# A trunk's FFN up-projections as seven products of quarters in place of eight

## The chip, the cores and the metric

The kernel runs on one core of a Trainium2 chip, as one launch. The metric is device time in microseconds, the median of several executions. TensorE multiplies matrices into PSUM; VectorE and ScalarE do element-wise work and can read PSUM; GpSimd does element-wise work on SBUF; SyncE issues the loads of the weights.

## The reference

The trunk has four layers on 512 tokens of 1024 features: retention, conv FFN, stick-breaking attention, conv FFN, each behind an RMS norm and added to x, with a norm at the end. All is float32. The change touches the conv FFN alone:

```python
def _conv_ffn(h, w_up, conv_w, conv_b, w_down):
    u = h @ w_up
    u = lax.conv_general_dilated(u, conv_w[:, None, :].astype(u.dtype), window_strides=(1,),
                                 padding=[(CONV_W - 1, 0)], ...,
                                 feature_group_count=2 * D_FF) + conv_b
    gate, val = jnp.split(u, 2, axis=-1)
    return (jax.nn.silu(gate) * val) @ w_down
```

`w_up` is 1024 x 5632 (gate and value, 2816 columns each), `w_down` 2816 x 1024, and the convolution is causal, of width 3, on every feature by itself.

## The kernel before, in words

Activations lie feature-major: a tile has 128 features in its partitions and the 512 tokens in its columns. x is eight such tiles. Every operand of a large product is held as a pair, `hi` (float32 cut to 12 significant bits) and `lo` (what is left), and a product is three matmuls, hi·hi, hi·lo and lo·hi (`mm3`, lines 106 to 111).

Weights come as a stream of chunks of 128 x 1024 floats (`chunk`, lines 94 to 104): SyncE loads a `raw` tile (three buffers), ScalarE casts `hi`, VectorE subtracts to get `lo` (four buffers each). A projection of a chunk (`proj`, line 134) takes 8 k tiles x 3 matmuls of 512 columns into one PSUM tile `acc` (three buffers).

An FFN (`ffn`, lines 394 to 403) has 22 feature tiles of gate and 22 of value. `first4` (line 117) does the first four of these 44 tiles with the k tiles outermost, so that they start while the norm is still being summed; half-way, `rsqrt` (line 183) makes `r`, the norm's factor per token, which ends with VectorE's RECIPROCAL on line 192. The factor is multiplied in behind the product: `up` (line 367) has VectorE multiply the PSUM tile by `r`, ScalarE take the last tap of the convolution and VectorE the two others (lines 374 to 377). `ffn_act` (line 380) has ScalarE's Silu, VectorE's product and a `split` into hi and lo. After 8, 16 (or 14) and 22 (or 18) features a part of the down-projection follows (`down`, lines 388 to 392): 8 output tiles of up to 24 matmuls of 512 columns, each added to x by VectorE.

The program is written in this order, and a scheduler sets the order on each engine at build time, by its own priorities and by which buffers come free; on the chip each engine then works strictly in that order. Waits are semaphores between engines. GpSimd does next to nothing: constants, and one-column memsets in the attention.

## Time and profile before

| | |
|---|---|
| time, median of 3 runs | 1389.64 us (1389.42 to 1390.57) |
| span of the profiled execution | 1387.6 us |
| that execution's own time | not listed apart; the runs' median is 2.0 us above the span |
| TensorE matmul busy | 1375.7 us, 99% of the span, 6668 instructions |
| VectorE busy | 940.1 us, 68%, 1282 instructions |
| ScalarE busy | 592.6 us, 43%, 867 instructions |
| GpSimd busy | 6.8 us, 69 instructions |
| read from HBM | 123.67 MB, 91 GB/s over the span |
| mean granted TensorE clock | 0.998 of full speed |

Times in the profile are microseconds unless marked ns. PE is TensorE's matmul row, PEld its weight loads, DVE is VectorE, ACT ScalarE, POOL GpSimd, SP SyncE. L103 is line 103 of the kernel. Matmul durations overlap: a matmul's row lasts longer than the distance to the next one's start, so their cost is read from starts. "out<-in" are the program's tile names without their numbers.

### The profile page before, as it was taken

What the parts mean: (1) busy time and instruction counts of PE and PEld (TensorE: products, weight loads), DVE (VectorE), ACT (ScalarE), POOL (GpSimd) and SP (SyncE); (2) the same over time, 40 slices, a digit from 0 to 9 for tenths busy, and PEclk for the clock granted to TensorE, in tenths of its full rate; (3) what the DMA queues carried; (4) which work ended last, traced back from release to release, by engine and by line L of the source; (5) the groups of instructions that cost most, each with busy time, mean ns of one, the idle gap of its engine ahead of it and who ended that gap; (6) DMA issues with size and microseconds to landing.
All of it is one profiled execution on the core that took longest, in us unless ns stands there. A gap on an engine that the chain in (4) does not pass through costs nothing.

```text
span 1387.6 us, 17028 instructions
## 1 busy us (share of the span) xinstructions
PE 1375.7 (99%) x6668; PEld 1140.9 (82%) x6668; DVE 940.1 (68%) x1282; ACT 592.6 (43%) x867; POOL 6.8 (0%) x69
## 2 busy tenths in 40 slices
PE   9999999999999999999999999999999999999997
PEld 7888888888888888888888888787788888888887
DVE  7774564654669773676367779889788753765765
ACT  5443332433355441443244655554355432433434
POOL 0000000000000000000000000000000000000000
PEclk9999999999999999999999999999999999999999
DMA  8233133131324333233322431120133233223221
GB/s 266 72 93 105 56 106 107 50 102 61 91 84 127 94 93 105 92 98 100 91 84 69 122 92 52 57 72 25 56 105 123 92 94 103 84 86 120 72 95 62
DMA packets 41025, 126.88 MB, mean 91 GB/s; under 512 B 4592, under 2 KB 6768, under 8 KB 40944
## 3 DMA queue, kind: packets, MB, share of 16 engines
q1 hardware_dynamic: 39424, 124.45, 29.0%
q10 hardware_dynamic: 1520, 1.33, 0.3%
q8 instruction: 53, 0.87, 0.3%
q14 instruction: 28, 0.23, 0.1%
HBM read 123.67 MB, written 2.10 MB: 91 GB/s over the span
## 4 chain that ended last, share of the span: by engine, by line
PE 96%; DVE 3%; ACT 0%; issue 0%; DMA 0%; DVEq 0%; ACTq 0%
PE acc L109 22%; PE acc L111 22%; PE acc L110 22%; PE att L109 8%; PE att L110 8%; PE att L111 8%; PE one L484 2%; PE z L458 1%; PE tp L476 1%; DVE cs L464 1%; DVE lo L103 1%; DVE tt L430 0%; DVE tt L427 0%; PE one L188 0%; PE one L223 0%
## 5 line engine op out<-in xcount | busy, mean ns | idle before, releaser
L102 ACT CAST hi<-raw 128x1024 fp32r<-128x1024 f32 (+2 forms) x253 | 244.6, 968 | 389.2 <-PE acc L110 182.0
L110 PE MATMUL acc<-xl,hi 128*128 128x512 f32 x960 | 374.6, 390 | 0.0
L111 PE MATMUL acc<-xh,lo 128*128 128x512 f32 x960 | 374.2, 390 | 0.0
L109 PE MATMUL acc<-xh,hi 128*128 128x512 f32 x960 | 374.2, 390 | 0.0
L103 DVE TENSOR_TENSOR lo<-raw,hi 128x1024 fp32r<-128x1024 f32 (+2 forms) x253 | 281.9, 1115 | 46.6 <-ACT hi L102 38.0
L111 PEld LDWEIGHTS acc<-xh,lo 128*128 128x128 f32 x960 | 180.2, 188 | 38.0 <-issue 0.5
L109 PEld LDWEIGHTS acc<-xh,hi 128*128 128x128 f32 x960 | 180.2, 188 | 36.6 <-issue 0.5
L110 PEld LDWEIGHTS acc<-xl,hi 128*128 128x128 f32 x960 | 180.3, 188 | 36.0
L377 DVE SCALAR_TENSOR_TENSOR tt<-tt,vec,tt 128x511 f32<-128x511 f32 (+1 forms) x176 | 131.2, 747 | 4.0 <-ACT tt L375 1.1
L374 DVE TENSOR_TENSOR tt<-acc,rr 128x512 f32<-128x512 f32 x80 | 55.0, 687 | 85.5 <-PE acc L111 85.5
L161 DVE TENSOR_TENSOR x<-x,att 128x512 f32<-128x512 f32 x40 | 27.4, 686 | 91.8 <-PE att L111 91.8
L109 PE MATMUL acc<-yy,hi 128*128 128x512 f32 x224 | 87.7, 392 | 0.1
L110 PE MATMUL acc<-yy,hi 128*128 128x512 f32 x224 | 87.6, 391 | 0.0
L111 PE MATMUL acc<-yy,lo 128*128 128x512 f32 x224 | 87.5, 391 | 0.0
L111 PE MATMUL acc<-hi,xl 128*128 128x512 f32 (+1 forms) x256 | 86.0, 336 | 0.0
L110 PE MATMUL acc<-lo,xh 128*128 128x512 f32 (+1 forms) x256 | 85.9, 336 | 0.0
L109 PE MATMUL acc<-hi,xh 128*128 128x512 f32 (+1 forms) x256 | 85.9, 336 | 0.0
L375 ACT ACTIVATE tt<-tt,vec 128x512 f32<-128x512 f32 x88 | 71.6, 814 | 7.5 <-DVE tt L374 6.4
L161 DVE TENSOR_TENSOR x<-x,acc 128x512 f32<-128x512 f32 x64 | 43.3, 684 | 43.2 <-PE acc L111 43.0
L111 PE MATMUL att<-yy,lo 128*128 128x512 f32 (+1 forms) x176 | 65.1, 370 | 0.0
L109 PE MATMUL att<-yy,hi 128*128 128x512 f32 (+1 forms) x176 | 65.1, 370 | 0.0
L110 PE MATMUL att<-yy,hi 128*128 128x512 f32 (+1 forms) x176 | 65.1, 370 | 0.0
(162 smaller groups left out, 1958.6 us busy)
## 6 DMA issues: line engine op xcount, KB each, us to landing
raw<-in_up SPq DMA_DIRECT2D x80, 512.0 KB, 3.6
raw<-in_down SPq DMA_DIRECT2D x24, 512.0 KB, 3.6
raw<-in_rv SPq DMA_DIRECT2D x16, 512.0 KB, 3.9
raw<-in_rg SPq DMA_DIRECT2D x16, 512.0 KB, 3.7
raw<-in_rout SPq DMA_DIRECT2D x16, 512.0 KB, 3.6
raw<-in_rqk SPq DMA_DIRECT2D x12, 512.0 KB, 3.7
raw<-in_down SPq DMA_DIRECT2D x16, 384.0 KB, 3.0
raw<-in_sqk SPq DMA_DIRECT2D x12, 512.0 KB, 3.7
```

Source lines behind the costliest of these rows:

```text
L102: nc.scalar.copy(hi, raw)
L103: nc.vector.tensor_sub(lo, raw, hi.bitcast(F32))
L109: mm(out, a[0], b[0], start=start, stop=False)
L110: mm(out, a[0], b[1], start=False, stop=False)
L111: mm(out, a[1], b[0], start=False, stop=stop)
L161: self.nc.vector.tensor_add(self.x[m], self.x[m], ps)
L374: nc.vector.tensor_mul(u, ps, self.r)
L375: nc.scalar.activation(c, u, AF.Identity, scale=w[2], bias=w[3])
L377: nc.vector.scalar_tensor_tensor(c[:, i:], u[:, : S - i], w[2 - i], c[:, i:], op0=ALU.mult, op1=ALU.add)
L458: nc.tensor.matmul(z[:, :nz], q[:, i * P : (i + 1) * P], k[:, :nz], start=m == 0, stop=m == 1)
L464: nc.vector.tensor_tensor_scan(left[:, :n][:, ::-1], sg[:, :n][:, ::-1], self.diag[:, S - n :][:, ::-1], 0.0, op0=ALU.mult, op1=ALU.max,)
L484: self.nc.tensor.matmul(o[e * DH : (e + 1) * DH, i * P : (i + 1) * P], v[p // 4 * NT + j][:, h * DH : (h + 1) * DH], aT[e][:, j * P : (j + ...
```

## The change

In each FFN the first four features (8 of 44 output tiles) stay as they were. The other 18 features are done two at a time, 9 blocks a layer. In a block the weights of a feature's gate and value tile (256 columns, 1024 k) are split in quarters: w11 (gate, first half of k), w12 (gate, second half), w21 and w22 (value). x, normed, is split into quarters by k halves and token halves. The four quarters of the output then come from seven products of sums of quarters, not eight (Winograd's form of Strassen's scheme): each product is 4 k tiles x 3 matmuls of 256 columns for each of the two features.

- `operands` makes the sums of x once a layer: ScalarE multiplies by the gain, GpSimd by `r` (8 tiles of 512 columns), GpSimd makes four differences of 256 columns for each of four pairs of k tiles, and ScalarE and VectorE split them into `oh` and `ol`, 7 x 256 columns each. So `r` is now needed ahead of the products.
- `pairs` makes a block. GpSimd adds the weight quarters: w21+w22, w21+w22 combined with w11, then with w12, and w11+w21 (the host stores the quarters with the signs that make these plain sums). Each sum is split like a chunk. Eight quarters are loaded a block, since w11, w21, w12 and w22 are each needed twice.
- ScalarE and VectorE combine the products out of PSUM into the tiles `u` (five buffers), 256 columns at a time. Two products accumulate on top of one another in the PSUM tiles `x` and `z`.
- Down-projections use `acc` throughout; tiles of a phase come from a pool of that phase.

```diff
+STD = 4
+Q = HALF
...
     def chunk(self, c, cols=CH):
         nc = self.nc
         raw = self.raw()
+        nc.sync.dma_start(raw[:, :cols], c)
+        return self.parts(raw, cols)
+
+    def parts(self, raw, cols=CH):
+        nc = self.nc
         hi = self.wp.tile([P, CH], F32R, tag="hi", bufs=4, name=self.name("hi"))
         lo = self.wp.tile([P, CH], F32R, tag="lo", bufs=4, name=self.name("lo"))
         raw, hi, lo = raw[:, :cols], hi[:, :cols], lo[:, :cols]
-        nc.sync.dma_start(raw, c)
         nc.scalar.copy(hi, raw)
         nc.vector.tensor_sub(lo, raw, hi.bitcast(F32))
...
+    T1, T3, T2, T4, X21, X22, X11 = range(7)
+
+    def operands(self, which):
+        nc, r = self.nc, self.r
+        self.ops = []
+        for i in range(KD // 2):
+            xn = []
+            for m in (i, i + KD // 2):
+                g = self.vec[:, which * KD + m : which * KD + m + 1]
+                y = self.sb("uu")
+                nc.scalar.activation(y, self.x[m], AF.Copy, scale=g)
+                nc.gpsimd.tensor_mul(y, y, r)
+                xn.append(y)
+            (x11, x12), (x21, x22) = [(y[:, :Q], y[:, Q:]) for y in xn]
+            ta, tb = self.sb("tt"), self.sb("tt")
+            t1, t3, t2, t4 = ta[:, :Q], ta[:, Q:], tb[:, :Q], tb[:, Q:]
+            nc.gpsimd.tensor_sub(t1, x12, x11)
+            nc.gpsimd.tensor_sub(t3, x12, x22)
+            nc.gpsimd.tensor_sub(t2, x22, t1)
+            nc.gpsimd.tensor_sub(t4, x21, t2)
+            hi, lo = self.sb("oh", 7 * Q, F32R), self.sb("ol", 7 * Q, F32R)
+            for n, src in ((self.T1, ta), (self.T2, tb), (self.X21, x21), (self.X22, x22), (self.X11, x11)):
+                c = slice(n * Q, n * Q + src.shape[1])
+                if n >= self.X22:
+                    nc.scalar.mul(hi[:, c], src, -1.0)
+                    nc.vector.scalar_tensor_tensor(lo[:, c], src, -1.0, hi[:, c].bitcast(F32), op0=ALU.mult, op1=ALU.subtract)
+                else:
+                    nc.scalar.copy(hi[:, c], src)
+                    nc.vector.tensor_sub(lo[:, c], src, hi[:, c].bitcast(F32))
+            self.ops.append((hi, lo))
+
+    def quarter(self, out, w, p, n, start):
+        mm = self.nc.tensor.matmul
+        for k in range(4):
+            c, o = slice((4 * p + k) * P, (4 * p + k + 1) * P), slice(n * Q, (n + 1) * Q)
+            a, b = [x[:, c] for x in w], [x[:, o] for x in self.ops[k]]
+            for i, (ai, bi) in enumerate(((0, 0), (0, 1), (1, 0))):
+                mm(out[:, :Q], a[ai], b[bi], start=start and k + i == 0, stop=k == 3 and i == 2,
+                   skip_group_check=not start)
+
+    def pairs(self, name, block):
...
+        def add(raw, c):
+            other = self.raw()
+            nc.sync.dma_start(other, c)
+            nc.gpsimd.tensor_add(raw, raw, other)
...
+        w = self.parts(raw)
+        for p in range(2):
+            self.quarter(x[p], w, p, self.X11, True)
+            nc.scalar.mul(u[p][0][:, :Q], x[p][:, :Q], -1.0)
+        add(sums, w22)
+        add(raw, w21)
+
+        w = self.parts(sums)
+        for p in range(2):
+            self.quarter(z[p], w, p, self.T1, True)
+            nc.scalar.copy(u[p][1][:, Q:], z[p][:, :Q])
+        add(sums, w11)
+
+        w = self.parts(sums)
+        for p in range(2):
+            self.quarter(x[p], w, p, self.T2, False)
+            nc.scalar.mul(u[p][0][:, Q:], x[p][:, :Q], -1.0)
+        add(sums, w12)
+        w = self.chunk(w12)
+        for p in range(2):
+            y = self.acc()
+            self.quarter(y, w, p, self.X21, True)
+            nc.vector.tensor_add(u[p][0][:, :Q], u[p][0][:, :Q], y[:, :Q])
...
     def ffn(self, l, last):
         a, s = [], 0
         first = self.first4(f"ufirst{l}")
-        for f in range(NF):
-            a.append(self.ffn_act(l, f, first[2 * f : 2 * f + 2] if f < 2 else (None, None)))
-            if s < 2 and f == STAGES[l][s][1] + 1:
+        self.phase("ffn")
+        self.operands(1 + 2 * l)
+        for f in range(STD):
+            ps = first[2 * f : 2 * f + 2] if f < 2 else (None, None)
+            a.append(self.ffn_act(f, self.up(l, f, ps[0]), self.up(l, NF + f, ps[1])))
...
+        for f in range(STD, NF, 2):
+            for p, (g, v) in enumerate(self.pairs(f"pairs{l}", (f - STD) // 2)):
+                a.append(self.ffn_act(f + p, self.conv(l, f + p, g), self.conv(l, NF + f + p, v)))
+            if s < 2 and f + 1 > STAGES[l][s][1]:
                 self.down(l, a, s, None)
                 s += 1
```

The three products left out of `pairs` go the same way: raw (w11+w21) with T3, sums with X22, a chunk w22 with T4.

How the order on the engines moves. First VectorE behind the reciprocal that ends the norm of layer 0's FFN (`att` are first4's PSUM tiles, `acc_664` that of feature 2's gate, `lo_677` and `lo_683` the lo of feature 3's chunks). Before:

```order
L192 RECIPROCAL rr_639_3214<-tt_638_3212 128x512
L103 TENSOR_TENSOR lo_663_3320<-raw_661_3318,hi_662_3319 128x1024
L103 TENSOR_TENSOR lo_669_3357<-raw_667_3355,hi_668_3356 128x1024
L374 TENSOR_TENSOR tt_649_3282<-att_616_3123,rr_639_3214 128x512
L103 TENSOR_TENSOR lo_677_3400<-raw_675_3398,hi_676_3399 128x1024
L377 SCALAR_TENSOR_TENSOR tt_650_3283<-tt_649_3282,vec_70,tt_650_3283 128x511
L374 TENSOR_TENSOR tt_651_3288<-att_617_3124,rr_639_3214 128x512
L377 SCALAR_TENSOR_TENSOR tt_650_3283<-tt_649_3282,vec_70,tt_650_3283 128x510
L374 TENSOR_TENSOR tt_655_3300<-att_618_3125,rr_639_3214 128x512
L377 SCALAR_TENSOR_TENSOR tt_652_3289<-tt_651_3288,vec_70,tt_652_3289 128x511
L103 TENSOR_TENSOR lo_683_3437<-raw_681_3435,hi_682_3436 128x1024
```

Now, from the same reciprocal on (`lo_689` and `lo_695` are feature 2's, `ol` the lo of the operands):

```order
L219 RECIPROCAL rr_640_3217<-tt_639_3215 128x512
L130 TENSOR_TENSOR lo_689_3424<-raw_687_3421,hi_688_3423 128x1024
L130 TENSOR_TENSOR lo_695_3461<-raw_693_3458,hi_694_3460 128x1024
L454 TENSOR_TENSOR ol_656_3302<-uu_652_3292,oh_655_3301 128x256
L454 TENSOR_TENSOR ol_656_3302<-tt_653_3295,oh_655_3301 128x512
L451 SCALAR_TENSOR_TENSOR ol_656_3302<-uu_652_3292,oh_655_3301 128x256
L454 TENSOR_TENSOR ol_656_3302<-tt_654_3296,oh_655_3301 128x512
L451 SCALAR_TENSOR_TENSOR ol_656_3302<-uu_651_3289,oh_655_3301 128x256
L454 TENSOR_TENSOR ol_662_3326<-tt_659_3319,oh_661_3325 128x512
```

20 such splits follow one another, with three products of `att` by `r` among the last; then come taps and sums of features 0 to 2, and among the last of these the lo of feature 3's gate and value:

```order
L399 TENSOR_TENSOR uu_691_3452<-acc_690_3427,rr_640_3217 128x512
L409 SCALAR_TENSOR_TENSOR tt_684_3411<-uu_683_3409,vec_73,tt_684_3411 128x511
L108 TENSOR_TENSOR aa_680_3400<-tt_678_3393,aa_679_3399 128x512
L409 SCALAR_TENSOR_TENSOR tt_684_3411<-uu_683_3409,vec_73,tt_684_3411 128x510
L409 SCALAR_TENSOR_TENSOR tt_692_3454<-uu_691_3452,vec_73,tt_692_3454 128x511
L415 TENSOR_TENSOR tt_684_3411<-tt_682_3405,tt_684_3411 128x512
L409 SCALAR_TENSOR_TENSOR tt_692_3454<-uu_691_3452,vec_73,tt_692_3454 128x510
L399 TENSOR_TENSOR uu_697_3489<-acc_696_3464,rr_640_3217 128x512
L108 TENSOR_TENSOR aa_686_3418<-tt_684_3411,aa_685_3417 128x512
L130 TENSOR_TENSOR lo_703_3504<-raw_701_3501,hi_702_3503 128x1024
L409 SCALAR_TENSOR_TENSOR tt_698_3491<-uu_697_3489,vec_73,tt_698_3491 128x511
L130 TENSOR_TENSOR lo_709_3541<-raw_707_3538,hi_708_3540 128x1024
```

So feature 3's two lo stood 4th and 10th behind the reciprocal, and now stand 43rd and 45th, behind all splits and most of the convolutions of three features. Layer 1 has the same order.

Second, GpSimd in two blocks one behind the other, where it had nothing:

```order
L478 TENSOR_TENSOR sums_724_3593<-sums_724_3593,raw_728_3627 128x1024
L478 TENSOR_TENSOR raw_725_3594<-raw_725_3594,raw_729_3630 128x1024
L478 TENSOR_TENSOR sums_724_3593<-sums_724_3593,raw_732_3663 128x1024
L478 TENSOR_TENSOR sums_724_3593<-sums_724_3593,raw_735_3696 128x1024
L478 TENSOR_TENSOR sums_764_3861<-sums_764_3861,raw_768_3895 128x1024
L478 TENSOR_TENSOR raw_765_3862<-raw_765_3862,raw_769_3898 128x1024
L478 TENSOR_TENSOR sums_764_3861<-sums_764_3861,raw_772_3931 128x1024
L478 TENSOR_TENSOR sums_764_3861<-sums_764_3861,raw_775_3964 128x1024
```

Four adds a block, three of them on one tile, with that tile's split by ScalarE and VectorE between one add and the next.

Third, VectorE where one block's taps meet the next block's products (`lo_814` to `lo_818` belong to the third and fourth product of the later block, `tt` and `uu` to the earlier one):

```order
L130 TENSOR_TENSOR lo_814_4203<-sums_804_4129,hi_813_4202 128x1024
L409 SCALAR_TENSOR_TENSOR tt_789_4097<-uu_757_3854,vec_73,tt_789_4097 128x511
L409 SCALAR_TENSOR_TENSOR tt_789_4097<-uu_757_3854,vec_73,tt_789_4097 128x510
L409 SCALAR_TENSOR_TENSOR tt_792_4107<-uu_758_3855,vec_73,tt_792_4107 128x511
L415 TENSOR_TENSOR tt_789_4097<-tt_788_4093,tt_789_4097 128x512
L409 SCALAR_TENSOR_TENSOR tt_792_4107<-uu_758_3855,vec_73,tt_792_4107 128x510
L409 SCALAR_TENSOR_TENSOR tt_793_4111<-uu_759_3856,vec_73,tt_793_4111 128x511
L108 TENSOR_TENSOR aa_791_4104<-tt_789_4097,aa_790_4103 128x512
L409 SCALAR_TENSOR_TENSOR tt_793_4111<-uu_759_3856,vec_73,tt_793_4111 128x510
L130 TENSOR_TENSOR lo_818_4238<-raw_816_4235,hi_817_4237 128x1024
```

Between two lo of weights stand eight instructions of the block before, where five stood between two chunks' lo in the up-projections before.

## Rows read from the trace of the kernel before

**Rows 1.** The page: span, busy time by engine, chain that ended last.

```profile
span 1387.6 us, 17028 instructions
...
PE 1375.7 (99%) x6668; PEld 1140.9 (82%) x6668; DVE 940.1 (68%) x1282; ACT 592.6 (43%) x867; POOL 6.8 (0%) x69
...
PE 96%; DVE 3%; ACT 0%; issue 0%; DMA 0%; DVEq 0%; ACTq 0%
```

**Rows 2.** Busy time by stretches, two FFN phases; first line names the columns.

```profile
core 0: us, PE busy (x) PEld busy (x) DVE busy (x) ACT busy (x) POOL busy (x), PEclk, DMA share, GB/s
402.00:728.00 326.00, 326.00 (x1440) 269.87 (x1439) 207.77 (x257) 129.28 (x156) 0.00 (x0) 1.00 0.33 100
1006.00:1320.00 314.00, 314.00 (x1386) 259.79 (x1385) 212.14 (x271) 130.83 (x166) 0.00 (x0) 1.00 0.32 98
```

**Rows 3.** Timeline, TensorE, up-projection: start, length, what; first, last of 51.

```profile
1319.64 0.39 PE L109 MATMUL acc<-xh,hi 128*128 128x512 f32 x1
...
1330.97 0.39 PE L111 MATMUL acc<-xh,lo 128*128 128x512 f32 x1
```

**Rows 4.** Timeline, TensorE, last down-projection by halves: first, last of 84.

```profile
1355.83 0.28 PE L109 MATMUL att<-vv,hi 128*128 128x256 f32 x1
...
1365.79 0.28 PE L111 MATMUL att<-yy,lo 128*128 128x256 f32 x1
```

**Rows 5.** Timeline, VectorE, first features of layer 0's FFN.

```profile
425.99 0.68 DVE L374 TENSOR_TENSOR tt<-att,rr 128x512 f32<-128x512 f32 x1
426.59 0.74 DVE L377 SCALAR_TENSOR_TENSOR tt<-tt,vec,tt 128x511 f32<-128x511 f32 x1
427.25 1.21 DVE L103 TENSOR_TENSOR lo<-raw,hi 128x1024 fp32r<-128x1024 f32 x1
428.38 0.74 DVE L377 SCALAR_TENSOR_TENSOR tt<-tt,vec,tt 128x510 f32<-128x510 f32 x1
```

**Rows 6.** Groups by line, VectorE: line, operation, shapes, count, busy us, mean ns.

```profile
L103 DVE TENSOR_TENSOR lo<-raw,hi 128x1024 fp32r<-128x1024 f32 x193 | 235.6, 1221 | 31.3 <-ACT hi L102 26.7 <-PE att L110 1.5
...
L377 DVE SCALAR_TENSOR_TENSOR tt<-tt,vec,tt 128x510 f32<-128x510 f32 x88 | 65.8, 748 | 2.7
...
L384 DVE TENSOR_TENSOR tt<-tt,tt 128x512 f32<-128x512 f32 x44 | 30.4, 690 | 1.3
...
L568 DVE TENSOR_TENSOR x<-x,att 128x256 f32<-128x256 f32 x16 | 6.7, 417 | 6.1 <-PE att L111 5.6
```

**Rows 7.** Groups by line, ScalarE.

```profile
L102 ACT CAST hi<-raw 128x1024 fp32r<-128x1024 f32 x193 | 203.2, 1053 | 319.6 <-PE acc L110 157.8 <-PE att L110 121.6 <-issue 17.5
...
L375 ACT ACTIVATE tt<-tt,vec 128x512 f32<-128x512 f32 x88 | 71.6, 814 | 7.5 <-DVE tt L374 6.4
...
L383 ACT ACTIVATE tt<-tt 128x512 f32<-128x512 f32 x44 | 27.8, 632 | 72.2 <-DVE tt L377 71.9
...
L460 ACT ACTIVATE pp<-z 128x256 f32<-128x256 f32 x16 | 6.2, 385 | 24.4 <-PE z L458 14.7 <-DVE tt L421 9.5
```

**Rows 8.** Groups by line, GpSimd.

```profile
L463 POOL MEMSET cs<- 128x1 f32 x64 | 6.3, 98 | 975.5 <-DVE pp L468 646.0 <-DVE pp L291 278.4 <-DVE tt L236 50.7
L225 POOL TENSOR_SCALAR_AFFINE_SELECT diag<-diag 128x128 f32<-128x128 f32 x1 | 0.3, 292 | 1.2 <-DVE diag L219 1.2
```

**Rows 9.** The page: GB/s in 40 slices, loads of up-projection weights.

```profile
GB/s 266 72 93 105 56 106 107 50 102 61 91 84 127 94 93 105 92 98 100 91 84 69 122 92 52 57 72 25 56 105 123 92 94 103 84 86 120 72 95 62
...
raw<-in_up SPq DMA_DIRECT2D x80, 512.0 KB, 3.6
```

**Rows 10.** Timeline, VectorE: the reciprocal ending the norm, both layers.

```profile
415.42 3.35 DVE L192 RECIPROCAL rr<-tt 128x512 f32<-128x512 f32 x1 [1.31 <-ACT tt L190]
...
1030.86 3.35 DVE L192 RECIPROCAL rr<-tt 128x512 f32<-128x512 f32 x1 [2.39 <-ACT tt L190]
```

**Rows 11.** Timeline, TensorE: first matmul of feature 2, both layers.

```profile
424.17 0.39 PE L109 MATMUL acc<-xh,hi 128*128 128x512 f32 x1
...
1037.44 0.39 PE L109 MATMUL acc<-xh,hi 128*128 128x512 f32 x1
```

More of the change, by code (lines that the diff above doesn't have):

```diff
@@ L55, in swap_pool, with phase @@
         self.att_pool()
+    def phase(self, which):
+        if self.pp is not None:
+            self.pp.__exit__(None, None, None)
+            self.pp = None
+        if which:
+            self.pp = self.tc.tile_pool(name=self.name(which), bufs=1, reuse_waits="tile")
+            self.ph = self.pp.__enter__()
     def name(self, s):
@@ new lines, in quarter @@
+    def quarter(self, out, w, p, n, start):
[7 more added lines that the diff above has]
+    def pairs(self, name, block):
+        nc, t = self.nc, self.t[name][block]
+        w11, w12, w21, w22 = t[0], t[1], t[2], t[3]
+        u = [[self.sb("uu") for _ in range(2)] for _ in range(2)]
+        x = [self.psum("x", 2) for _ in range(2)]
+        z = [self.psum("z", 2) for _ in range(2)]
+        def add(raw, c):
+            other = self.raw()
+            nc.sync.dma_start(other, c)
+            nc.gpsimd.tensor_add(raw, raw, other)
+        sums = self.wp.tile([P, CH], F32, tag="sums", bufs=2, name=self.name("sums"))
+        raw = self.raw()
+        nc.sync.dma_start(raw, w11)
+        nc.sync.dma_start(sums, w21)
+        w = self.parts(raw)
[19 more added lines that the diff above has]
+            nc.vector.tensor_add(u[p][0][:, :Q], u[p][0][:, :Q], y[:, :Q])
+        w = self.parts(raw)
+        for p in range(2):
+            self.quarter(x[p], w, p, self.T3, False)
+            nc.vector.tensor_add(u[p][1][:, Q:], u[p][1][:, Q:], x[p][:, :Q])
+        w = self.parts(sums)
+        for p in range(2):
+            self.quarter(z[p], w, p, self.X22, False)
+            nc.vector.tensor_sub(u[p][0][:, Q:], u[p][0][:, Q:], z[p][:, :Q])
+        w = self.chunk(w22)
+        for p in range(2):
+            self.quarter(x[p], w, p, self.T4, False)
+            nc.scalar.copy(u[p][1][:, :Q], x[p][:, :Q])
+        return u
@@ L638, in _token_major, with _pairs @@
     )
+def _pairs(rows):
+    w = np.stack(rows).reshape(2, 2, 4, P, 2, P)
+    return w.transpose(0, 1, 3, 4, 2, 5).reshape(4, P, 2 * 4 * P)
 def _columns(v):
@@ L673, in _layout @@
         a[f"ufirst{l}"] = np.concatenate(first, 1).reshape(KD, P, S)
-        a[f"up{l}"] = _rows(np.concatenate([g[:, 2 * P :], v[:, 2 * P :]], 1), KD, P)
+        rest = [m[:, f * P : (f + 1) * P] for f in range(2, STD) for m in (g, v)]
+        a[f"up{l}"] = _rows(np.concatenate(rest, 1), KD, P)
+        a[f"pairs{l}"] = np.stack([_pairs([m[:, f * P : (f + 2) * P] for m in (g, v)]) for f in range(STD, NF, 2)])
         for s, (lo, hi) in enumerate(STAGES[l]):
```

35 lines of the change are left out of this document (22 added, 13 removed).

## The prediction

> **What bounds the kernel now.** I read the page's busy shares and the chain that ended last first: TensorE is busy for 99% of the span and is 96% of the chain [rows 1]. The busy time by stretches says the same of the two FFN phases: TensorE is busy in every microsecond at a granted clock of 1.00 (its 2.4 GHz level), VectorE for about two thirds, GpSimd not at all [rows 2]. So time is won by fewer or cheaper matmuls and lost by anything that makes TensorE wait. Busy time of matmuls overlaps, so I take their price from the timeline, start to start: 50 steps of a 512-column matmul in 11.33 us, 0.2266 us each [rows 3], and 83 steps of a 256-column one, each with its own weight load, in 9.96 us, 0.1200 us each [rows 4].
>
> **Sum 1, matmuls.** A pair of features (4 output tiles) took 4 x 24 matmuls of 512 columns, 21.75 us. It now takes 7 products x 2 features x 12 matmuls of 256 columns, 168 x 0.1200 = 20.16 us. That is 7.3% less, not the 12.5% of the products' count, since half a matmul costs more than half. 18 pairs x 1.59 us = **28.7 us gained**, the most that the change can give, since down-projections, attention and the first four features keep their instructions.
>
> **Sum 2, VectorE inside a block.** Its instructions overlap a little, so again start to start: a lo of 1024 columns 1.13 us, a 512-column sum 0.60, a convolution tap 0.66 [rows 5], each about 0.08 below its duration [rows 6]. A 256-column sum out of PSUM lasts 0.417 [rows 6], so I take 0.34. A block has 7 lo (7.9), 6 sums out of PSUM (2.0), 8 taps (5.3) and 4 sums of 512 (2.4): 17.6 us in 20.16. Before it was 4 lo, 8 taps and 8 sums of 512, 14.6 in 21.75. VectorE fits, with 2.5 us spare. ScalarE has 7 casts, 8 moves of 256 columns out of PSUM, 4 taps, and 2 Silu and 2 splits at a Silu's price: 7.4 + 3.1 + 3.3 + 2.5 = 16.3 us [rows 7], hidden.
>
> **Sum 3, GpSimd.** No row shows it adding two tiles. The nearest is its AFFINE_SELECT, 0.292 us for 128 columns, beside 0.098 for one column [rows 8]. Scaled by columns, an add of 1024 takes 2.34 us, one of 512 1.17, one of 256 0.58. VectorE's own durations (1.22, 0.69, 0.42) [rows 6] are the lower end; the upper end is a second operand at the row's rate of 1.53 ns per column, 3.2, 1.66 and 0.88. I take the scaled row. Four adds a block are 9.4 us of 20.16, ahead of need: sums have two buffers. The Trainium skill's "GPSIMD Engine Reference", section "Performance versus the Vector engine", has 4497 ns for 2048 columns; by it an add of 1024 would be an estimated 2.25 us, and the sum would not change.
>
> **Sum 4, weights.** A block loads 8 chunks of 512 KB where 4 were; 4.2 MB in 20.16 us are 208 GB/s, under the 266 GB/s of the first slice [rows 9]. One of three raw buffers holds w11 for nearly a whole block. The other two carry six transfers of 3.6 us [rows 9] and their reader of some 2.3: 36 of 40 us. Hidden, but little is left.
>
> **Sum 5, the operands.** This I expect to cost most. VectorE works in program order. Behind the reciprocal that ends the norm it has two lo and then the splits of the sums of x, which wait for GpSimd: 8 products of 512 and 16 differences of 256, one chain of 8 x 1.17 + 16 x 0.58 = 18.7 us, which cannot start before the reciprocal is done. Behind the last split (ScalarE's cast 0.62, then three lo, 1.3) stand 10 taps and 7 sums for features 0 to 2, 6.6 + 4.2, and only then the lo of feature 3's gate chunk, 1.13: 13.9 us. TensorE waits for that lo. The reciprocal ends at 415.42 + 3.35 = 418.8 in layer 0 and at 1034.2 in layer 1 [rows 10], so the lo is there at 451.4 and 1066.8. TensorE starts feature 2 at 424.2 and 1037.4 [rows 11] and is done with it 10.9 us later, and has eight more matmuls (1.4 us) that don't need the lo. It stands still from 436.5 and 1049.7: **14.9 + 17.1 = 32.0 us lost.** With VectorE's durations as GpSimd's the chain is 12.2 us and the two stalls are 8.4 + 10.6 = 19.0; with the upper prices the chain is 27.4 and they are 23.6 + 25.8 = 49.4. Before, nothing waited: the taps were free to follow the reciprocal. No row of before shows TensorE's clock at its lower level, 1.2 GHz; if it falls in such a stall, each adds a little.
>
> **Sum 6, two engines on SBUF.** GpSimd never reads SBUF beside a busy VectorE before, so no row shows whether they hinder one another. Bounds: nothing; or every instruction of VectorE with two SBUF operands waits while GpSimd adds, and the other way round. In a block that is 7.9 + 5.3 + 2.4 = 15.6 us of VectorE and 9.4 of GpSimd, 25.0 us, 4.8 over TensorE's 20.16. It is paid where the taps of one block meet the products of the next. Blocks stand in groups of 3, 4, 2 and 3, 3, 3 between down-projections, so there are 12 such meetings, 58 us; a group's last taps run under a down-projection. In the operands' stage the splits and two lo, 9.4 us, would lengthen GpSimd's chain twice, 19 us. Together 0 to 77 us. No row is nearer to either end; I take half, **38 us**.
>
> **The sum.** The profiled span is 1387.6 us [rows 1], the median of the runs 1389.64, so 2.0 us lie around it; all changes are against the median. 1389.6 - 28.7 + 32.0 + 38 = **1431 us**, slower. Free of cost: down-projections out of three accumulators in place of four (the sum into x takes 0.69 of the 5.4 us of a tile), and the new pools, whose tiles were read long before.
>
> **Rivals.** *Faster, about 1380.* GpSimd's chain is short and hinders nobody. It decides at a chain of 16.4 us (14.4 us of stall a layer, half of 28.7); at VectorE's prices 1389.6 - 28.7 + 19.0 = 1380. For it: 128 columns in 0.292 us contain a fixed part. Against it: two operands are read, each step waits for the one before, and 13.9 us of VectorE stand behind the chain whatever GpSimd does. 18%.
>
> *No hindrance, GpSimd as priced:* 1389.6 - 28.7 + 32.0 = 1393, give or take 6. For it: VectorE has 2.5 us spare a block. 17%.
>
> *Full exclusion:* the upper end of sum 6, 1389.6 - 28.7 + 32.0 + 77 = 1470. For it: VectorE is 87% busy in a block, so an add nearly always meets an instruction; against it, some waits for TensorE would absorb adds. 25%. The Trainium skill has this as a rule ("SBUF — State Buffer", section "Who interferes with whom"): a VectorE instruction with two SBUF inputs and a GpSimd instruction that reads SBUF share a port, and the later one waits until the other has ended. No run here shows it yet; by it the sum is 1470, without it 1393.
>
> *My forecast,* part of that cost, 1405 to 1455: 40%.
>
> **The numbers.** A measurement of this kernel can tell about 0.2% (2.8 us) from no change. Faster takes the first rival less what lies within 2.8 us: 0.16. Same takes the rest of it and the lower part of the second: 0.08. Slower: 0.76. The range goes from 1377, just under the first rival's time, to 1473, just over the third's, leaving out a GpSimd yet faster (0.05) or a stall at the upper prices together with full exclusion (0.10). The forecast's own range is 1405 to 1455.
>
> **What would show it.** Right: 256-column matmuls 0.120 apart inside a block; one gap of 10 to 25 us in TensorE's row per layer, in the fourth feature, ended by VectorE's lo; GpSimd adds of 1024 near 2.3 us; VectorE's lo longer than 1.22 us or with gaps while GpSimd adds; blocks behind the first of a group longer than 20.2 us. Wrong: no gap in the operands' stage (then sum 5 fails, and 1365 to 1380 would come), GpSimd adds beside VectorE at unchanged durations of both (sum 6 is nothing), or TensorE waiting for raw buffers (sum 4).

## The result, and the profile after

The changed kernel takes **1491.74 us** (1489.98 to 1492.63 in 4 runs) against 1390.11 for the kernel before on the same chip: **slower, ratio 1.073 [1.0715, 1.0746]**, above the range of the forecast. The profiled span is 1488.2 us, 100.6 more than in [rows 1]. Where [rows 1] had TensorE busy for 99% of the span and 96% of the chain, the page now has (span; busy time; granted clock in 40 slices; chain):

```profile
span 1488.2 us, 20343 instructions
...
PE 1380.2 (93%) x7964; PEld 1203.9 (81%) x7964; DVE 1101.2 (74%) x1412; ACT 707.4 (48%) x1121; POOL 241.8 (16%) x189
...
PEclk9999999999987999989999999999977899999999
...
PE 42%; issue 33%; DVE 11%; POOL 7%; ACT 4%; DMA 3%; DVEq 0%; POOLq 0%; ACTq 0%; SPq 0%
```

TensorE waits, and around its waits the clock is down: 0.50 of full speed, which is 1.2 GHz, from 450 to 460 us, where it had mostly stood still, 0.75 around a wait between blocks, and 1.00 in a block that nothing hinders. What it waits for (waits by engine, TensorE; us in total, times, longest), and three stretches of the windows, with the columns of [rows 2]:

```profile
PE x L464 <- ACT uu L522: 43.3, 12, 5.5
PE x L464 <- ACT hi L129: 26.1, 2, 18.6
PE acc L138 <- DVE lo L130: 9.3, 2, 5.0
PE acc L136 <- ACT hi L129: 8.6, 1, 8.6
PE acc L136 <- DVE uu L399: 3.8, 2, 2.0
PE x L464 <- ACT uu L488: 3.4, 2, 2.0
```

```profile
450.00:460.00 10.00, 2.44 (x6) 1.43 (x6) 9.47 (x16) 7.78 (x12) 0.00 (x0) 0.50 0.00 0
...
495.00:505.00 10.00, 4.70 (x23) 4.50 (x22) 9.37 (x6) 5.62 (x9) 7.05 (x3) 0.75 0.33 105
...
592.00:612.00 20.00, 20.00 (x167) 19.93 (x166) 13.37 (x13) 9.03 (x13) 5.84 (x3) 1.00 0.57 177
```

The first line of the waits is at 12 places: the first product of each block that directly follows another. The rest, some 52 us, is in the two operand stages. VectorE's groups answer to [rows 6], GpSimd's to [rows 8]:

```profile
L130 DVE TENSOR_TENSOR lo<-raw,hi 128x1024 fp32r<-128x1024 f32 x193 | 253.0, 1312 | 42.9 <-ACT hi L129 41.6
L409 DVE SCALAR_TENSOR_TENSOR tt<-uu,vec,tt 128x510 f32<-128x510 f32 x88 | 93.4, 1065 | 1.2
L130 DVE TENSOR_TENSOR lo<-sums,hi 128x1024 fp32r<-128x1024 f32 x54 | 87.2, 1615 | 29.1 <-ACT hi L129 29.1
```

```profile
L478 POOL TENSOR_TENSOR sums<-sums,raw 128x1024 f32<-128x1024 f32 x54 | 137.7, 2550 | 387.7 <-DMA raw<-in_pairs 316.0 <-DVE lo L130 71.7
...
L437 POOL TENSOR_TENSOR uu<-uu,rr 128x512 f32<-128x512 f32 x16 | 26.2, 1642 | 469.6 <-DVE rr L219 467.8 <-ACT uu L436 1.8
```

A tap takes 1065 ns where it took 748, the lo of a sum 1615 where a lo took 1221. One meeting of two blocks in the timeline (GpSimd, VectorE, ScalarE, TensorE; start, length, what; in brackets the idle time before and what ended it):

```profile
494.11 2.37 POOL L478 TENSOR_TENSOR raw<-raw,raw 128x1024 f32<-128x1024 f32 x1 [3.76 <-DVE uu L517]
496.44 2.79 POOL L478 TENSOR_TENSOR sums<-sums,raw 128x1024 f32<-128x1024 f32 x1
...
494.45 5.32 DVE L409 SCALAR_TENSOR_TENSOR tt<-uu,vec,tt 128x511 f32<-128x511 f32 x2 [0.55 <-ACT tt L407]
...
499.25 1.04 ACT L129 CAST hi<-sums 128x1024 fp32r<-128x1024 f32 x1 [4.83 <-POOL sums L478]
500.21 0.37 ACT L522 COPY uu<-x 128x256 f32<-128x256 f32 x1
...
500.62 0.58 PE L464 MATMUL x<-oh,hi 128*128 128x256 f32 x1 [5.30 <-ACT uu L522]
```

Two taps, some 1.4 us of work by [rows 5], last 5.32 beside two adds that follow each other. ScalarE works in order: its cast waits for the second add, and behind that cast stands the copy that frees the PSUM tile `x` for TensorE.

Why the adds came so late is read from the chain that ended last, in the same stretch (start, length, what):

```profile
483.80 4.08 DMA raw<-in_pairs
...
487.96 2.41 POOL sums L478
...
490.38 3.48 DMA raw<-in_pairs
...
494.11 1.04 POOL raw L478
...
496.44 2.80 POOL sums L478
```

The first transfer was issued as VectorE's lo freed a raw buffer, the second as the add ahead of it freed one; the next add waited for each. So the three raw buffers stand in the chain too, though TensorE never waits for one directly.

**Where 100.6 us lie.** A block's length is read from TensorE's timeline, from the end of the step before it to its last matmul. All runs below have blocks right behind a down-projection at 20.14 to 20.16 us, the 168 x 0.1200 of the forecast. "Blocks" is what the 16 blocks that are not first in their layer take over 16 x 20.16 us; "rest" is the span's difference to before, plus 28.7, less "blocks": the two operand stages with the first blocks, and anything else. In e9 the blocks hold the added matmuls.

| run | time, us | ratio to before | blocks | rest |
|---|---|---|---|---|
| the changed kernel | 1491.7 | 1.073 [1.0715, 1.0746] | 67.0 | 62.3 |
| e1_tiny_adds | 1421.8 | 1.0232 [1.0217, 1.0247] | 2.3 | 57.8 |
| e2_x3 | 1485.3 | 1.0687 [1.0671, 1.0703] | 60.6 | 62.7 |
| e5_no_pool | 1387.8 | 0.9986 [0.9977, 0.9995] | 1.8 | 23.6 |
| e6_dve_adds | 1453.4 | 1.0459 [1.0444, 1.0475] | 32.4 | 58.8 |
| e7_dma_adds | 1473.1 | 1.0593 [1.0576, 1.0611] | 52.1 | 60.8 |
| e8_ops_dve | 1480.2 | 1.0648 [1.0632, 1.0664] | 64.8 | 52.0 |
| e9_filler | 1507.5 | 1.0842 [1.0821, 1.0863] | 87.4 | 59.9 |
| e10_ops_front | 1480.5 | 1.0651 [1.0634, 1.0668] | 67.3 | 49.5 |
| e11_mix | 1421.2 | 1.0229 [1.0212, 1.0246] | 21.4 | 37.2 |
| e13_long_adds | 1437.4 | 1.034 [1.0319, 1.0361] | 14.7 | 58.2 |
| e14_long_ops | 1464.6 | 1.0539 [1.0522, 1.0557] | 69.7 | 34.3 |
| e15_adds_then_sets | 1443.1 | 1.0386 [1.0369, 1.0403] | 23.7 | 58.2 |
| e16_ops_then_sets | 1481.9 | 1.066 [1.0644, 1.0676] | 74.4 | 47.3 |

Two runs on the kernel before (e3, e4) and e12, which has 16 blocks, are told below. Of the 67.0 us, 46.5 are waits and some 21 are matmuls further apart than 0.120 us behind a wait (the two overlap a little).

### The profile page after: what moved, and what is told of

Its sections match the earlier page's. It is cut to its first block, busy times and chain, and to the rows that moved or that the text cites. A ratio compares the mean times of both kernels' runs of the same rounds, so it can differ in the third digit from the quotient of the medians.

```text
span 1488.2 us, 20343 instructions
## 1 busy us (share of the span) xinstructions
PE 1380.2 (93%) x7964; PEld 1203.9 (81%) x7964; DVE 1101.2 (74%) x1412; ACT 707.4 (48%) x1121; POOL 241.8 (16%) x189
## 4 chain that ended last, share of the span: by engine, by line
PE 42%; issue 33%; DVE 11%; POOL 7%; ACT 4%; DMA 3%; DVEq 0%; POOLq 0%; ACTq 0%; SPq 0%
PE acc L136 8%; PE acc L138 8%; PE acc L137 7%; PE x L464 7%; POOL sums L478 4%; DVE lo L130 4%; PE z L464 3%; DMA raw<-in_pairs 3%; DVE tt L409 2%; ACT hi L129 2%; PE acc L464 2%; PE one L625 1%; PE z L599 1%; POOL uu L437 1%; PE tp L617 1%
## 5 line engine op out<-in xcount | busy, mean ns | idle before, releaser
L464 PE MATMUL x<-oh,hi 128*128 128x256 f32 x576 | 174.7, 303 | 73.7 <-ACT uu L522 43.3
L136 PE MATMUL acc<-xh,hi 128*128 128x512 f32 x512 | 202.6, 396 | 12.4 <-ACT hi L129 8.6
L138 PE MATMUL acc<-xh,lo 128*128 128x512 f32 x512 | 201.5, 394 | 9.3 <-DVE lo L130 9.3
L137 PE MATMUL acc<-xl,hi 128*128 128x512 f32 x512 | 202.4, 395 | 0.0
L478 POOL TENSOR_TENSOR sums<-sums,raw 128x1024 f32<-128x1024 f32 x54 | 137.7, 2550 | 387.7 <-DMA raw<-in_pairs 316.0
L464 PEld LDWEIGHTS x<-oh,hi 128*128 128x128 f32 x576 | 119.3, 207 | 78.7 <-ACT uu L522 45.7
L409 DVE SCALAR_TENSOR_TENSOR tt<-uu,vec,tt 128x510 f32<-128x510 f32 (+1 forms) x176 | 171.1, 994 | 11.4 <-ACT tt L407 9.8
L464 PE MATMUL x<-ol,hi 128*128 128x256 f32 x576 | 171.9, 298 | 0.0
L464 PE MATMUL x<-oh,lo 128*128 128x256 f32 x576 | 170.9, 297 | 0.0
L464 PEld LDWEIGHTS x<-ol,hi 128*128 128x128 f32 x576 | 119.9, 208 | 0.2
L130 DVE TENSOR_TENSOR lo<-sums,hi 128x1024 fp32r<-128x1024 f32 x54 | 87.2, 1615 | 29.1 <-ACT hi L129 29.1
```

The lines of the kernel that those rows point to most:

```text
L130: nc.vector.tensor_sub(lo, raw, hi.bitcast(F32))
L136: mm(out, a[0], b[0], start=start, stop=False)
L137: mm(out, a[0], b[1], start=False, stop=False)
L138: mm(out, a[1], b[0], start=False, stop=stop)
L409: nc.vector.scalar_tensor_tensor(c[:, i:], u[:, : S - i], w[2 - i], c[:, i:], op0=ALU.mult, op1=ALU.add)
L464: mm(out[:, :Q], a[ai], b[bi], start=start and k + i == 0, stop=k == 3 and i == 2, skip_group_check=not start)
```

## Experiments on the hindrance itself

The theory: VectorE's instructions with two SBUF operands and GpSimd's additions take turns. The main rival: only the order of waits costs.

**Additions beside the kernel before (e3_side_adds).**

```diff
+            w = self.wchunk(f"up{l}", f - 2 - 2 * (f // NF))
+            nc.gpsimd.tensor_copy(self.sc[:, :1], w[0][:, :1].bitcast(F32))
+            for _ in range(2):
+                nc.gpsimd.tensor_add(self.sc, self.sc, w[0].bitcast(F32))
...
```

> The kernel before, with two GpSimd additions of 1024 columns beside each up-projection chunk, into a tile that nobody reads; a copy of one column ties them to the chunk's arrival. Nothing else waits for them except the hi buffer that they read. Theory (exclusion: work of VectorE with both operands from SBUF and GpSimd's additions do not run at once): per chunk of 5.44 us of TensorE, VectorE has about 2.5 us of such work and GpSimd 4.7 us, some 7.9 us with the waits between; VectorE's taps and lo subtractions lengthen (747 and 1221 ns before) and the time grows by 100 to 240 us. Rival (the delays of the changed kernel are waits in its order, not a hindrance between the engines): within 5 us of the kernel before, VectorE's durations as before.

1576.7 us, ratio 1.1351 [1.1332, 1.137]: 187 us, with nobody waiting for the sums. VectorE's groups, one line of GpSimd's, and TensorE's first matmul of two features that follow each other:

```profile
L383 DVE SCALAR_TENSOR_TENSOR tt<-tt,vec,tt 128x510 f32<-128x510 f32 x88 | 162.7, 1848 | 2.7
...
L390 DVE TENSOR_TENSOR tt<-tt,tt 128x512 f32<-128x512 f32 x44 | 83.7, 1902 | 1.3
L380 DVE TENSOR_TENSOR tt<-acc,rr 128x512 f32<-128x512 f32 x80 | 54.5, 682 | 6.6 <-PE acc L111 6.6
```

```profile
L375 POOL TENSOR_TENSOR sc<-sc,hi 128x1024 f32<-128x1024 f32 x160 | 446.1, 2788 | 12.7
```

```profile
1226.15 0.76 PE L109 MATMUL acc<-xh,hi 128*128 128x512 f32 x1 [4.81 <-DVE tt L380]
...
1243.99 0.76 PE L109 MATMUL acc<-xh,hi 128*128 128x512 f32 x1 [4.81 <-DVE tt L380]
```

A tap went from 748 to 1848 ns; the product with one operand in PSUM (L380) stayed at 682. The period is 17.84 us, where TensorE needs 10.88. By [rows 5], VectorE's part with two SBUF operands is 2 lo, 4 taps and 2 sums, 6.1 us; four adds at 2.37 are 9.5; with the two products out of PSUM, 1.2, it makes 16.8, and the rest, 1.0, is near the two small copies (0.76 each on average). That is nearly one engine after the other, as the theory has it. This run and the next also set the transfers' scratch smaller.

**Fills beside the kernel before (e4_side_sets).**

```diff
-                nc.gpsimd.tensor_add(self.sc, self.sc, w[0].bitcast(F32))
+                nc.gpsimd.memset(self.sc, 0.0)
...
```

> As the run with side additions, but GpSimd fills the tile (memset of 1024 columns, twice per chunk) in place of adding: it writes as many columns and reads none. If the hindrance is of reading two operands, as the exclusion theory has it, the time stays within 5 us of the kernel before and VectorE's taps near 747 ns; if any GpSimd work on SBUF hinders VectorE, it grows in proportion to the sets' busy time, by 30 us or more.

1389.8 us, ratio 1.000 [0.999, 1.0009]:

```profile
L383 DVE SCALAR_TENSOR_TENSOR tt<-tt,vec,tt 128x510 f32<-128x510 f32 x88 | 65.9, 749 | 2.7
```

153 us of fills cost nothing (nor does the smaller scratch), so what hinders comes with GpSimd's reading. The Trainium skill, "SBUF — State Buffer", section "Who interferes with whom", says both: a VectorE instruction with two SBUF inputs contends with a GpSimd instruction that reads SBUF, not with one that only writes it. These two runs agree.

**Short adds in the changed kernel (e1_tiny_adds, then e13_long_adds and e15_adds_then_sets).**

```diff
-            nc.gpsimd.tensor_add(raw, raw, other)
+            nc.gpsimd.tensor_add(raw[:, :8], raw[:, :8], other[:, :8])
```

> The changed kernel with GpSimd's weight adds on 8 of their 1024 columns: 99% of the weight sums are left out, every wait and the order on every engine stay. Theory (reading time): the 12 meetings of the changed kernel, 43.3 us of TensorE waiting for ScalarE's copy out of PSUM, exist because an add of 2.55 us stands still beside VectorE's work and the two adds of a cast follow one another; with adds of a fraction of a us they go, and the clock that fell in them comes back in part (about 24 us were lost in the whole kernel). The operands' stage (some 52 us) stays, since its small products and subtractions are untouched. Time 1425 to 1450 us; VectorE's taps back from 994 ns to near 750. Rival (order alone): the casts come late because of what is issued ahead of them, however short the adds: 1470 us or more, and the same waits of TensorE for ScalarE.

1421.8 us, just under the theory's range: the meetings went (0.7 us of L522 waits are left of 43.3), taps are at 745 ns, the stage stayed. The theory's side, but this edit shortens the adds and removes their reading at once. Two runs part these.

```diff
+            for _ in range(2):
+                nc.gpsimd.memset(other[:, 8:], 0.0)
             nc.gpsimd.tensor_add(raw[:, :8], raw[:, :8], other[:, :8])
```

> The changed kernel with each weight add made of two GpSimd fills of 1016 columns (0.95 us each) of the tile just read, and an add of 8 columns: GpSimd takes about as long (2.3 us) before a sum is ready, but hardly reads; 99% of the weight sums are left out. ScalarE's order differs from the changed kernel's by swaps of neighbouring instructions. Theory (turns: VectorE is held up while GpSimd adds): without the reading adds VectorE is not held up, the blocks lose most of the 67 us by which the 16 that are not first in their layer exceed 20.16 us each, and the time is 1422 to 1442 us. Rival (length: a sum comes 2.4 us later than a cast wants it, whatever VectorE does): blocks keep most of their excess, 1465 us or more.

1437.4 us, blocks 14.7. But fills that wait for nothing were done ahead, so the length was not wholly kept. With the fills behind the add, in the tile that the cast waits for:

```diff
             nc.gpsimd.tensor_add(raw[:, :8], raw[:, :8], other[:, :8])
+            for n in (CH, CH, 256):
+                nc.gpsimd.memset(raw[:, :n], 0.25)
```

> The changed kernel with each weight add on 8 of 1024 columns, followed by fills of the same tile (two of 1024 columns and one of 256, 2.2 us), so that the cast waits for the add and the fills, which cannot be done ahead: the length of GpSimd's part in the chain of a sum is now kept in full (in the run with fills ahead of the add, some fills were done before their turn). Weight sums are left out but for 8 columns. Theory (GpSimd's reading holds VectorE up and the other way round): the blocks keep at most a third of their 67 us, time 1425 to 1445 us. Rival (the length of the adds in the chain): blocks keep over two thirds, 1465 us or more; between the two, both.

1443.1 us, blocks 23.7, with GpSimd busier than in the changed kernel (254.7 us against 241.8) and taps at 746 ns. So of the blocks' 67.0 us about **43 go when GpSimd hardly reads** and **24 stay with the length** (2.3 of them stay without the adds too, e1): a third, the edge of what the theory allowed.

That the 43 are all hold-up is not shown. This edit frees the buffer of the second quarter behind the add of 8 columns, not behind the fills, so the next transfer is issued some 2 us sooner (timeline of e15; in the chain above it started at 490.38, behind an add of 2.41):

```profile
486.01 0.20 POOL L478 TENSOR_TENSOR sums<-sums,raw 128x8 f32<-128x8 f32 x1 [5.86 <-DMA raw<-in_pairs]
486.24 0.80 SPq L477 DMA_DIRECT2D raw<-in_pairs  x2
```

e13 keeps the length up to that release and costs 12.4 us more than e1; e15 keeps it up to the cast and costs 21.4 more. If the two simply add, which is an estimate, 34 are length and 31 hold-up; so the hold-up is some 31 to 43 us. About 14 of the 43 are narrower spacing of the matmuls again, 29 are waits. The scheduler also set some 160 of ScalarE's 1121 instructions in another order, and a fourth raw buffer, which would tell more, was not run.

**Adds on VectorE (e6_dve_adds).** `nc.gpsimd.tensor_add(raw, raw, other)` becomes `nc.vector.tensor_add(raw, raw, other)`.

> The changed kernel with the 72 weight adds on VectorE in place of GpSimd, everything else as it was. Theory (GpSimd's additions and VectorE's two-operand SBUF work take turns): an add on GpSimd costs VectorE's turn 2.4 us, on VectorE 1.22 us (the lo subtraction's duration, the same shape), so a block's 25 us of turns become 17.6 + 4 x 1.22 = 22.5 us against 20.2 us of TensorE; of 1421.8 us without the adds, 18 blocks x 2.3 us = 42 us at most come back, less where the down-projections let VectorE catch up: 1425 to 1465 us, faster than the changed kernel. Rival (the engines run side by side and only the order of waits costs): VectorE gets 88 us more work that GpSimd carried, and the time grows past 1495 us.

1453.4 us, as the theory had it: VectorE does the adds in 1219 ns each and the kernel is 38 us faster than with GpSimd doing them. This does not part hold-up from length, since an add is also half as long.

**Adds by the transfer (e7_dma_adds).**

```diff
-            other = self.raw()
-            nc.sync.dma_start(other, c)
-            nc.gpsimd.tensor_add(raw, raw, other)
+            nc.gpsimd.dma_start(raw, c, accum_op=ALU.add)
```

> The changed kernel with the weight sums formed by the transfer itself: the second quarter is brought by a DMA from GpSimd's queue that adds to the tile, in place of a DMA into another buffer and a GpSimd add. If an adding transfer lands as a plain one does (3.6 us for 512 KB) and hinders no engine, the time is that of the kernel with adds of 8 columns, 1415 to 1430 us (the operands' stage keeps its 52 us). If the adding transfers are slow (over 8 us each: four in a block of 20 us, one behind the other for three of them), TensorE waits for casts of sums behind them, and the time is above 1450 us.

1473.1 us, above the 1450 expected only for transfers of over 8 us. Adding transfers land in 6.1 us at the median, plain ones in 4.3 (issues: queue, count, size, us to landing):

```profile
sums<-in_pairs POOLq DMA_DIRECT2D x54, 512.0 KB, 6.1
raw<-in_pairs SPq DMA_DIRECT2D x54, 512.0 KB, 4.3
```

VectorE is undisturbed (taps 746 ns), yet the casts come late, since three of a block's four adds go into one tile, each behind the lo of the sum before. It is the length again, without the hold-up.

**A third PSUM tile x (e2_x3).** `self.psum("x", 2)` becomes `self.psum("x", 3)`.

> The changed kernel with three PSUM buffers for the tile x in place of two; nothing else is edited. Theory A (what the meetings cost is the release of x, queued on ScalarE behind a cast that waits for GpSimd): the first product of a block no longer waits for the copy of the block before, the 43.3 us of waits for ScalarE's copy fall by more than half and the time to 1430 to 1460 us. Theory B (in a block VectorE and GpSimd together have more work than TensorE, so that the wait only moves): TensorE waits as long for another thing, the cast of a sum or the lo part of it; time 1475 us or more. In both the operands' stage keeps its 52 us.

1485.3 us; the L522 waits fall only to 31.1 us, and others come in their place. With three tiles the second feature of a block still needs the first one's tile of the block before, so the wait was not wholly removed. Nearer to theory B; four tiles were not run.

**Filling the waits (e9_filler).**

```diff
...
+        fill, o = FILLER[name].get(block, 0), None
+        for i in range(fill):
+            o = self.one() if o is None else o
+            nc.tensor.matmul(o[:, :Q], w[0][:, :P], self.ops[0][0][:, :Q], start=i == 0, stop=i == fill - 1)
```

> The changed kernel with matmuls of 256 columns into a PSUM tile that nobody reads, put ahead of a block's first product at the 12 places where TensorE waits there (11 to 38 of them, each some 85% of that place's wait in the changed kernel at 0.12 us apiece; 311 in all, 37 us): work added, nothing else moved. Theory (the lower granted clock after a wait costs time of its own, about 24 us in the whole kernel by the spacing of the matmuls of 256 columns that follow): the clock stays at its upper level there and the time falls by 8 to 20 us, although TensorE does 37 us more. Rival (the clock has nothing to do with the waits): the added work either fits the waits, 1488 to 1494 us, or lengthens the kernel by up to 37 us.

1507.5 us, a miss of the theory. With these matmuls in the program the scheduler set ScalarE's order differently (some 50 of its instructions moved), and 34 us of waits for ScalarE's copies remain beside the filling. It isolates nothing: what the lower clock costs by itself is read from the spacing, not shown by a run.

## Experiments on the operand stages

**The stage on VectorE (e8_ops_dve).** `nc.gpsimd.tensor_mul` and the four `nc.gpsimd.tensor_sub` of `operands` become `nc.vector`.

> The changed kernel with the operands' multiplications and subtractions (8 and 16 in each layer) on VectorE in place of GpSimd; the weight adds stay on GpSimd. Theory (turns): the 28.4 us of GpSimd's chain in a layer, lengthened from 18.7 + 9 us, become 8 x 0.69 + 16 x 0.42 = 12.2 us of VectorE with 13.9 us of lo parts after and between them; each layer's wait of TensorE falls by 10 to 16 us, the time to 1455 to 1475 us. Rival (the stage waits for VectorE's own queue, GpSimd's chain runs beside it): VectorE's chain grows by 12.2 us a layer and the time to 1500 to 1516 us.

1480.2 us: the right direction, half the size. TensorE now waits mostly for one eviction, queued behind VectorE's operands:

```profile
PE acc L136 <- DVE uu L399: 35.6, 2, 19.0
```

**The same, in another order (e10_ops_front).** Chunks and products of features 2 and 3 ahead, an eviction between two operand pairs:

```diff
...
+        ps = [self.proj(self.wchunk(f"up{l}", i), self.xs) for i in range(3)]
+        for i in range(4):
+            self.operands(1 + 2 * l, i)
+            us.append(self.sb("uu"))
+            self.nc.vector.tensor_mul(us[i], ps[i], self.r)
...
```

> The kernel with the operands' work on VectorE (1480.2 us), with the weights of features 2 and 3 and their products put ahead of the operands in the program, and the eviction of each product between two operand pairs. Weight adds stay on GpSimd. Theory: of the 20 to 22 us that TensorE still waits in each layer's operand stage, most is an eviction (16.6 and 19.0 us) that stands behind all four operand pairs on VectorE; with it moved between them TensorE finishes features 2 and 3 meanwhile and waits only for what VectorE's 26 us of operands exceed its cover of 22 us by: 5 to 10 us a layer, time 1450 to 1468 us. Rival (VectorE's total ahead of the first block decides, in whatever order): the wait moves to the first block, 1475 us or more.

1480.5 us, no change: the rival. The wait moved to the first block, as it would if VectorE's total ahead of it decides.

**Without GpSimd's adds as well (e11_mix).** First sum and the sum into w11 by adding transfers, the other two on VectorE.

> The kernel with the operands on VectorE and ahead in this way, and no weight add on GpSimd: of a block's four, the first sum and the sum into the first quarter are formed by adding transfers (each has a product or more of time), the two that follow a cast at once are VectorE's. VectorE then has 17.6 + 2 x 1.22 = 20.0 us in a block of 20.2 us of TensorE. By the theory of turns nothing collides any more; the matmul term (-27 us) comes through less 10 to 20 us of the operands' stage and some us of short waits and clock: 1383 to 1410 us. Rival (seven products bring short waits whoever adds, as with adding transfers alone): 1415 us or more.

1421.2 us, the rival's range, but the blocks' 21.4 us are the smaller part of it and the rest, 37.2, the larger. In the stage VectorE is busy in every microsecond, and in the second of these windows TensorE mostly stands:

```profile
434.00:444.00 10.00, 10.00 (x46) 8.28 (x45) 10.00 (x22) 7.12 (x13) 0.00 (x0) 1.00 0.32 54
444.00:454.00 10.00, 3.14 (x15) 2.20 (x13) 10.00 (x18) 5.12 (x9) 0.00 (x0) 0.82 0.14 52
```

**With six features as eight products (e12_mix6).** `STD = 4` becomes `STD = 6`.

> The same, with six feature tiles of a layer as eight products in place of four (one block fewer in each layer, 3 us of the matmul term), which gives TensorE 22 us more work while VectorE forms the operands. If the operands' stage is what is left of the loss, its waits fall below 5 us a layer and the time is 5 to 20 us under the mix with four: 1372 to 1395 us. If the loss lies in the blocks, it is within 4 us of it.

1417.0 us, ratio 1.0194 [1.0179, 1.021]: 4 us less, not the 5 to 20 hoped for. By the same reckoning with 16 blocks (25.4 us of the matmul term) the rest falls from 37.2 to 29.4 us, but 3.2 are lost again with the two blocks that went and 2.1 in the blocks that are left. So more cover helps the stage, and little is won in all; of all versions that compute the whole trunk it is the fastest, and still slower than the kernel before.

**The stage without reading (e14_long_ops, then e16_ops_then_sets).** Multiplications and subtractions on 8 columns, with fills ahead of each, then behind each:

```diff
+                for _ in range(2):
+                    nc.gpsimd.memset(ta, 0.0)
-                nc.gpsimd.tensor_mul(y, y, r)
+                nc.gpsimd.tensor_mul(y[:, :8], y[:, :8], r[:, :8])
...
```

> The changed kernel with the operands' multiplications and subtractions on 8 columns only (the rest left out), each after fills that bring it near its undisturbed length (two of 512 columns before a multiplication, one of 256 before a subtraction): GpSimd's chain in the operands' stage keeps nearly its length but hardly reads. Weight adds as in the changed kernel. Theory (turns): the stage loses what the two engines took from each other there, about 9 us a layer of the chain's 28.4, and some clock: 1465 to 1480 us. Rival (the stage is the sum of GpSimd's own chain and VectorE's lo parts, one behind the other): within 6 us of the changed kernel, 1486 us or more.

1464.6 us, rest 34.3. The fills ran ahead of the reciprocal, and GpSimd's chain shrank from 28.4 (418.55 to 446.94) to 14.1 us, so this is hold-up and length together.

```diff
+                nc.gpsimd.tensor_mul(y[:, :8], y[:, :8], r[:, :8])
+                for _ in range(2):
+                    nc.gpsimd.memset(y, 0.25)
...
```

> The changed kernel with the operands' multiplications and subtractions on 8 columns, each followed by fills of its own output (two of 512 columns; one of 256 and one of 128), so that what comes next waits for them: in the run with fills ahead, GpSimd's chain had shrunk from 28.4 to 14.1 us, here it should be near 19 to 21 us. The operands' values are left out but for 8 columns. Theory (reading): of the 62 us outside the blocks 35 to 48 stay, time 1462 to 1478 us. Rival (length alone): 1483 us or more.

1481.9 us, between the two by its time. The chain is 25.6 us, longer than meant; the rest is 47.3, but the blocks, with another order, take 7 us more. So in the stages the hold-up is some 15 us by this run and 28 by the run before, which also has the shorter chain. How much exactly stays open.

**No GpSimd work at all (e5_no_pool).** Short weight adds, and in `operands` neither multiplications nor subtractions.

> The changed kernel with GpSimd's work taken out: the weight adds on 8 of 1024 columns, the operands' multiplications by r and their subtractions left out (so neither the weight sums nor the operands' sums are formed; the products run on the unsummed tiles). All products, casts, lo parts and FFN work stay. If GpSimd's additions and what waits for them are all that the change cost, what is left is the forecast's matmul term alone, 1389.9 - 28.7 = 1361 us, plus a few us for VectorE's 14 us of operand lo parts: 1361 to 1375 us. If another part of the change costs (more transfers, short matmuls of 256 columns, PSUM buffers, the added evictions), it stays above 1385 us.

1387.8 us, 2 under the kernel before, and above the 1385 from which another part of the change had to cost something. That part is the split of the operands: the blocks are clean, but in the stage TensorE waits for VectorE's lo parts, and in all 23.6 us lie outside the blocks:

```profile
PE acc L138 <- DVE lo L130: 14.0, 2, 7.0
PE acc L136 <- ACT hi L129: 3.5, 1, 3.5
```

So even a GpSimd that cost nothing would leave 2 us of the 28.7.

## Why the prediction was wrong

- **Sum 1 (28.7 us)** was right: a block without hindrance takes 20.15 us, and with the adds out (e1, e5) nearly all do.
- **Sum 2** was right: VectorE fits a block when nothing holds it up (e1: blocks 2.3 us over in all).
- **Sum 3 is one of the two steps that failed.** It had the size of an add of 1024 columns (2.34; 2.37 in the meeting above), but counted its wait at nothing: "ahead of need: sums have two buffers". Three of four adds go into one tile, each behind the lo of the sum before it (71.7 us of GpSimd's idle time end with that lo), and ScalarE's next cast waits for it. The adds' length cost some 21 to 34 us in the blocks. The small steps were priced too low: the fastest product of 512 columns took 1.28 us (1.17 forecast), the fastest difference of 256 columns 0.72 (0.58).
- **Sum 4** held only in that no wait of TensorE ends with a raw buffer. Its "Hidden" did not: transfers into raw buffers are 3% of the chain that ended last, some 43 us, and the late adds above waited for them. What they cost alone stays open; with adds of 8 columns the same transfers leave the blocks at 20.16 us (e1).
- **Sum 5 (32.0 us)** named the stage and a part of its price. Outside the blocks 62.3 us were lost, 34 to 47 without the hold-up. I placed the wait at VectorE's lo of feature 3, 9.3 us of it; the larger waits end with ScalarE's casts, queued behind casts of operands that wait for GpSimd. Giving GpSimd's part to VectorE, in either order, left 52.0 and 49.5 us (e8, e10).
- **Sum 6 is the other step that failed:** "No row is nearer to either end; I take half, 38 us." The runs beside the kernel before show that the engines take turns, which is what the upper end assumed. In the changed kernel the hold-up is some 31 to 43 us in the blocks and 15 to 28 in the stages, 46 to 71 against the 77 of the upper end; that it comes so near is in part luck, since the blocks' figure contains the clock, which the 77 did not. The place was right: 12 meetings, those named, with 5.6 us each (67.0 / 12, lengths and clock included) against 4.8. A stage's chain of 28.4 us looks like full exclusion's 18.7 + 9.4, but that is luck too: at the fastest durations its own work is some 21 us, and 1.1 us are waits for ScalarE. The rule of the Trainium skill ("SBUF — State Buffer", section "Who interferes with whom"), told beside the third rival, agrees with the two runs beside the kernel before; I had that rival at 25%.
- **The clock** was named and not priced. Some 21 of the blocks' 67 us are matmuls spaced wider behind a wait, at a granted clock of 0.75 in the meeting above.
- **Taken together,** full exclusion alone gave 1470 us, 22 short of what was measured; the adds' length and the clock, both counted at nothing, carry the time past it. The corner that the range left out, upper prices with full exclusion, comes to 1389.6 - 28.7 + 49.4 + 77 = 1487 us, but an add took 2.4 us and not its 3.2, so that nearness is luck.
- **Two slips of the sums** change little: by its own numbers the first rival's chain is 17.0 us and not 16.4, and by sum 2's prices the splits (without the last three) and two lo of sum 6 are 9.9 us and not 9.4.

The forecast's +41 became +101: -28.7 as forecast, 67 in the blocks where it had 29 (half of 58), 62 in the stages where it had 41.5 (32.0 and half of 19).

## What to carry to other kernels

Work given to an idle GpSimd was not free beside a busy VectorE. Fills, which only write, were free, and VectorE's product with one operand in PSUM kept its 682 ns; but an addition of 2.4 us held up VectorE's work with two SBUF operands, and VectorE does the same addition itself in 1.22 us (1453 against 1492 us). Where a trace can't show whether two engines exclude each other, price both ends and ask which single run parts them: additions and then fills beside the unchanged kernel took two runs here. And look for what is queued behind a wait on an in-order engine: here a copy that frees PSUM stood behind a cast that waited for an add.

## What the runs showed of the hardware that was not expected

- GpSimd's fills of 1024 columns (0.95 us, 160 of them) left VectorE's durations and the time as they were.
- A transfer of 512 KB that adds to its destination lands in 6.1 us where a plain one in the same kernel took 4.3, and VectorE's taps stayed at 746 ns beside it.
- Short waits pull the clock down as well. In the run with adding transfers, a block with three waits of 2.4 us in all took 24.56 us, 2.2 of it wider spacing, at a granted clock of 0.93; a clean one has 1.00 (windows):

```profile
492.80:517.40 24.60, 22.72 (x171) 21.90 (x170) 18.26 (x25) 14.61 (x24) 3.46 (x4) 0.93 0.65 159
585.50:605.60 20.10, 20.10 (x169) 20.07 (x168) 11.79 (x15) 10.21 (x16) 3.25 (x4) 1.00 0.77 189
```
